# One order of matmul widths in every triple, and another way to fold the sample columns, in a one-core hybrid decoder step

## The chip, the core and the metric

The kernel runs on one core of one Trainium2 chip. TensorE (PE in the profile) multiplies, VectorE (DVE), ScalarE (ACT) and GpSimd (POOL) do everything else, and SyncE (SP) issues most of the DMAs. The metric is device microseconds of one execution, as a median over runs.

## What is computed

One layer of a decoder trunk is applied to 256 prompt tokens and 8 sample tokens (264 columns in all) with a model width of 2048. In fp32:

```
xn = rms_norm(x) ; z = xn @ w_in                      # 2048 -> 3584, columns split among three mixers
A: pooling over windows 2/4/8/16, a 128x128 map per group, @ w_pool_br
B: conv of width 4, RG-LRU (two 128x128 gate maps per block, a scan over time), * gelu gate, @ w_lru_br
C: GLU, conv of width 31, LayerNorm, silu, @ w_conf_br
x = x + (sum_b sigmoid(xn @ w_gate + b_gate)_b * y_b) @ w_out
x = x + relu(rms_norm(x) @ w_up)^2 @ w_down           # 2048 -> 8192 -> 2048
y = rms_norm(x)                                       # and the new mixer states
```

All of it is fp32, and every product is made from split operands, as the next section tells.

## The kernel before

**Layout.** Activations lie feature by feature: a k-tile is 128 features on the partitions and the 264 tokens along the row. `X` holds the residual stream. Every operand of a product is kept as a high part (the value rounded to fp32r) and a low part (the rest). Both lie side by side in one row, so `both(t, k)` is 528 columns wide: low prompt (0 to 255), low sample (256 to 263), high prompt (264 to 519), high sample (520 to 527). Low sample and high are thus neighbours.

**The triple.** A weight tile of 128x128 is also split, into `whi` and `wlo`. A product needs three matmuls: `whi` with the high activations, `whi` with the low ones, `wlo` with the high ones. `mm` and `mm3` (lines 234 to 242) make them so: k=0 is `whi` on columns 256 to 527 (low sample and all of high, 272 wide) into columns 0 to 271 of the PSUM bank; k=1 is `whi` on the low prompt (256 wide) into columns 8 to 263; k=2 is `wlo` on high (264 wide) into columns 8 to 271. So columns 8 to 271 of a bank hold the product, but for the product of the low sample part, which lies apart in columns 0 to 7. The order in a triple is 256, 272, 264. Only in the first triple of an accumulation is it 272, 256, 264, since the widest must clear the bank.

**Folding the sample columns.** `join` (line 158) adds columns 0 to 7 to the sample columns 264 to 271: ACT copies them to `side` in SBUF (L161), VectorE adds them back in PSUM (L162). Then the bank's consumer reads `tokens(ps)`, columns 8 to 271. Every accumulation has such a join, 288 in all.

**Order of the work.** The weights come as a list of chunks of 128x1024 (two k-tiles by 512 output features), in the order of `weight_plan`. A group is one weight matrix by 512 output features: 7 groups of w_in, 12 of w_gate, 4 each of w_pool_br, w_lru_br, w_conf_br and w_out, 16 of w_up and 16 of w_down, 67 in all. A group uses four PSUM banks, one for each of its four output tiles m, and the next group uses the other four. In each chunk the loops run over two k-tiles and four m, a triple each (`tile_mm`). The first four chunks go width by width instead (`by_operand`): four tiles with k=0, four with k=1, four with k=2. The small products are made between chunks: `lru_gate_mm` (four blocks of four products in "lru" chunks, with two sigmoids after each pair, L514 and L515) and `grp_mm` (four products, scaled by ACT in L767).

**Splitting of weights.** For chunk i+3 `split` is issued ahead of chunk i's matmuls: ACT casts `raw` to `whi` (L218), VectorE makes `wlo` from both (L219). `whi` and `wlo` have four buffers, `raw` six. Every engine works through its instructions in program order, so whatever an instruction waits for also delays the casts and subtractions queued behind it.

**Evacuation.** After a group's last chunk, for each m: `join`, then the consumer, for instance `gate_evac` (L792), `branch_evac` (L805, with additions on POOL in L808 and L811), `out_evac` (L831), `up_evac` (L866), `down_evac` (L892). Background stages (convolutions, gates, splits) are handed out between chunks by `run_bg` with a fixed credit for each engine; nothing in that depends on run time. The very last tile goes through `last_evac` (L888, L889), in two halves of 132 columns. Squares for the final norm are made by `square_add` on ACT (L854) and summed by POOL (L856), and the scaling by g_final is L897. The sums over the partitions are the matmuls of L1053.

Of the kernel before, what the change touches and what calls it, by code (L numbers as in the profile page):

```python
# [12 lines left out]
ALU = mybir.AluOpType  # L13
# [4 lines left out]
TP = 256  # L18
TS = 8
N = TP + TS  # L20
# [32 lines left out]
NHI = 4  # L53
# [38 lines left out]
def hybrid_step(ctx: ExitStack, tc: tile.TileContext, first, par_in, st_in, wall, y_out, st_out):  # L92
    nc = tc.nc
# [9 lines left out]
    whi = cpool.tile([P, NHI, CH], F32R, name="whi")  # L103
    wlo = cpool.tile([P, NHI, CH], F32R, name="wlo")
# [5 lines left out]
    L = cpool.tile([P, 8 * PITCH], F32R, name="L", tag="L")  # L110
    X = cpool.tile([P, KD, N], F32, name="X")
# [23 lines left out]
    def both(t, k):  # L135
        return part(t, k, 0, 2 * N)
# [16 lines left out]
    def tokens(ps):  # L153
        return ps[:, TS:TS + N]

    side, joined = cpool.tile([P, 4, TS], F32, name="side"), []

    def join(ps):
        t = side[:, len(joined) % 4, :]
        joined.append(t)  # L160
        nc.scalar.copy(t, ps[:, :TS])  # L161
        nc.vector.tensor_tensor(ps[:, N:N + TS], ps[:, N:N + TS], t, op=ALU.add)  # L162

    spare = nc.const_aps.tensor(1.0, [P, 2 * P], dtype=mybir.dt.bfloat16)
# [6 lines left out]
    groups, chunks = weight_plan()  # L171
# [59 lines left out]
        hi, lo, w = head_half(k, h)  # L231
        nc.vector.tensor_tensor(lo, w, f(hi), op=ALU.subtract)

    def mm(k, ps, w, x, start, stop=False):
        a, b = ((TP, 2 * N), (0, TP), (N, 2 * N))[k]
        o = (0, TS, TS)[k]
        nc.tensor.matmul(ps[:, o:o + b - a], w, x[:, a:b], start=start, stop=stop, skip_group_check=True)  # L237

    def mm3(ps, whi_t, wlo_t, x, first, last):
        for k in (0, 1) if first else (1, 0):  # L240
            mm(k, ps, whi_t, x, first and k == 0)
        mm(2, ps, wlo_t, x, False, last)

# [258 lines left out]
    def lru_gate_mm(ct, c, j):  # L504
        assert "xc" in done
        hi, lo = whi[:, c % NHI, :], wlo[:, c % NHI, :]
        out = []
        for t in range(2):
            s = slice((2 * j + t) * P, (2 * j + t + 1) * P)
            ps = acc()  # L510
            mm3(ps, hi[:, s], lo[:, s], both(L, ct), True, True)
            join(ps)
            out.append(ps)
        nc.scalar.activation(RA[:, ct, :], tokens(out[0]), AF.Sigmoid, bias=pv("b_lru_a", ct))  # L514
        nc.scalar.activation(TM[:, ct, :], tokens(out[1]), AF.Sigmoid, bias=pv("b_lru_x", ct))  # L515
        spend(act=1.0)
        if ct % 2:
            def times():
                nc.vector.tensor_tensor(XC[:, ct - 1:ct + 1, :], XC[:, ct - 1:ct + 1, :], TM[:, ct - 1:ct + 1, :],
                                        op=ALU.mult)  # L520
                spend(dve=0.71)

            later(1, times)
# [198 lines left out]
    def Q():  # L722
        if not q_at:
            q_at.append(cpool.tile([P, 8 * PITCH], F32R, name="Q", tag="Q"))
        return q_at[0]
# [33 lines left out]
    def grp_mm(c):  # L759
        assert "pool" in done  # L760
        hi, lo = whi[:, c % NHI, :], wlo[:, c % NHI, :]
        for gi in range(4):
            s = slice(gi * P, (gi + 1) * P)
            ps = acc()
            mm3(ps, hi[:, s], lo[:, s], both(Q(), gi), True, True)
            join(ps)
            nc.scalar.activation(DU[:, gi, :], tokens(ps), AF.Copy, scale=pv("pool_scale", gi))  # L767
        stage_split("pool", 2, lambda c: highs(Q(), 2 * c), lambda c: lows(Q(), 2 * c), lambda c: DU[:, 2 * c:2 * c + 2, :])
        mark("pool", "grp")
# [57 lines left out]

    sq2 = G[:, 20, :]

    def out_evac(m, ps):  # L830
        nc.vector.tensor_tensor(X[:, m, :], X[:, m, :], ps[:, :N], op=ALU.add)  # L831
        spend(dve=0.4)

        hi, lo = high(*bpart(m)), low(*bpart(m))

        def one():
            nc.scalar.activation(hi, X[:, m, :], AF.Copy, scale=pv("g_mlp", m))
            square_add(m)
            spend(act=0.8)

        def other():
            nc.vector.scalar_tensor_tensor(lo, X[:, m, :], pv("g_mlp", m), f(hi),
                                           op0=ALU.mult, op1=ALU.subtract)
            spend(dve=0.35)

        later(m % 4 // 2, one)
        later(m % 4 // 2 + 1, other)
        if m == KD - 1:
            later(4, lambda: total_fold(high(LH(), 0), G[:, 10, :], sq2))
            later(6, lambda: rms_close(high(LH(), 0)))  # L850
# [30 lines left out]
    def last_evac(whole):  # L881
        m = KD - 1
        for s in (slice(0, N // 2), slice(N // 2, N)):
            if s.start:
                join(whole)
            ps = tokens(whole)
            x = X[:, m, s]
            nc.vector.tensor_tensor(x, x, ps[:, s], op=ALU.add)  # L888
            nc.vector.tensor_tensor(G[:, 11, s], x, x, op=ALU.mult)  # L889

    def down_evac(q, m, ps):
        nc.vector.tensor_tensor(X[:, m, :], X[:, m, :], ps[:, :N], op=ALU.add)  # L892
        spend(dve=0.4)
        if q == 3:
            def rest():
                square_add(m, m < KD - 2)
                nc.scalar.activation(X[:, m, :], X[:, m, :], AF.Copy, scale=gfin[:, m:m + 1])  # L897

            later(0 if m >= KD - 4 else 1 + m % 4 // 2, rest)
# [51 lines left out]
    def by_operand(i, kt, rhs, pss):  # L951

        x = rhs(2 * i + kt)
        for k, w in enumerate((whi, whi, wlo)):
            for m in range(4):
                s = slice(kt * 512 + m * P, kt * 512 + (m + 1) * P)
                mm(k, pss[m], w[:, i % NHI, s], x, i == kt == k == 0)

    def tile_mm(i, c, kt, m, rhs, pss, stop):
        s = slice(kt * 512 + m * P, kt * 512 + (m + 1) * P)  # L960
        mm3(pss[m], whi[:, i % NHI, s], wlo[:, i % NHI, s], rhs(2 * c + kt), c == 0 and kt == 0, stop)


    for k in range(4):
# [13 lines left out]
    pss = None  # L978
    for i, ch in enumerate(chunks):
        now[0] = i  # L980
        if i < 5:
            x_tile(2 * i + 6)
            x_tile(2 * i + 7)
        for half in (0, 1) if i < 2 else (None,):
            split(i + AHEAD, half)
        if i == 12:
            softplus()
            again = first[:, KD:KD + 4 * HEAD].rearrange("p (k c) -> p k c", k=4)[:, :, :N]
            nc.sync.dma_start(X[:, 0:4, :], again)
            nc.vector.tensor_scalar(gfin, pv("g_final"), -0.5, None, op0=ALU.mult)  # L990
        if i % 2 == 0:
            dma_pair((i + 8) // 2)
        if i == 2:
            nc.sync.dma_start(par, par_in)
            nc.sync.dma_start(small(S_SMALL, S_IN - S_SMALL), st_in[:, S_SMALL:])
        if 13 <= i < 17:
            state_move(i - 13, lambda t, s: nc.sync.dma_start(t, st_in[:, s]))
        kind, gi, c, _ = ch
        if kind == "dense":
            rhs, fn = group(gi)  # L1000
            n = groups[gi][2] // 2
            if c == 0:
                pss = [acc() for _ in range(4)]
            if i < len(chunks) - 2:
                for kt in range(2):
                    if i < LEAD:
                        by_operand(i, kt, rhs, pss)
                    for m in range(4 * (i < LEAD), 4):
                        tile_mm(i, c, kt, m, rhs, pss, c == n - 1 and kt == 1)
            elif i == len(chunks) - 1:  # L1010
                for m in range(4):
                    for b in range(4):
                        tile_mm(i - 1 + b // 2, c - 1 + b // 2, b % 2, m, rhs, pss, b == 3)
            if c == n - 1:
                for m in range(4):
                    if (gi, m) == (len(groups) - 1, 3):
                        last_evac(pss[m])
                    else:
                        join(pss[m])
                        fn(m, tokens(pss[m]))  # L1020
                after(gi)
        elif kind == "lru":
            for j in range(2):
                lru_gate_mm(2 * gi + j, i, j)
            if gi == 3:
                lru_tail()
        elif kind == "grp":
            grp_mm(i)
        if i == len(chunks) - 4:
            nc.scalar.preload_act_table_set(ROOT)  # L1030
        if 136 <= i < 140:
            state_move(i - 136, lambda t, s: nc.sync.dma_start(st_out[:, s], t))
        if i == 140:
            nc.sync.dma_start(st_out[:, S_SMALL:], st)
        if 5 <= i < 9:
            x_squares(i - 5)
        if i == 9:
            later(0, x_sum)
        if i == 12:
            later(0, x_rms)  # L1040
        run_bg()
# [8 lines left out]
    ps = [acc(), acc()]  # L1050
# [139 lines left out]
```

## Time and profile before

| | us |
|---|---|
| median of 3 runs | 1386.58 (1385.03 to 1386.98) |
| the profiled execution | 1385.67 |
| its span, first to last instruction | 1383.9 |
| PE busy | 1367.4 (99%) |
| VectorE busy | 876.9 (63%) |
| ACT busy | 758.3 (55%) |
| GpSimd busy | 94.7 (7%) |

A row of the timeline view has the start and length in us, the engine, the line, the operation with output and inputs by the program's names, and a count where several were merged; in brackets stands the engine's idle time ahead of it and what ended that. A row of the groups of instructions has the busy time and the mean ns of one behind the first bar and the idle time behind the second. In the page's first part an engine's row has busy us, share of the span and instructions.

### The profile page before, as it was taken

The numbers are of one execution on the slowest core, as the hardware profiler recorded it, in microseconds if no ns is written. First come the engines' busy times: TensorE is split into PE (matmuls) and PEld (weight loads), VectorE is DVE, ScalarE is ACT, GpSimd is POOL, SyncE is SP. The second block draws the span as 40 slices with busy tenths as digits, with TensorE's granted clock in tenths as the row PEclk, the third lists the DMA queues.
The fourth block names the chain that finished last, engine by engine and source line by source line (L and its number), as shares of the span: only waits on it lengthen the run. The fifth ranks groups of instructions, "written<-read, shape, count | busy, mean of one in ns | idle before, by whom it ended". The sixth has DMA issues, their size and how long they took to land.

```text
span 1383.9 us, 27199 instructions
## 1 busy us (share of the span) xinstructions
PE 1367.4 (99%) x11421; PEld 1363.9 (99%) x11421; DVE 876.9 (63%) x1340; ACT 758.3 (55%) x1309; POOL 94.7 (7%) x125
## 2 busy tenths in 40 slices
PE   9999999999999999999999999999999999999996
PEld 9999999999999999999999999999999999999996
DVE  7786788776767668666655455655455655555554
ACT  7756667667665655555544344543344533454553
POOL 0230010110101013010000000000000000000012
PEclk9999999999999999999999999999999999999999
DMA  8654556555565554655555555555555555555551
GB/s 321 215 176 162 189 183 211 178 182 192 183 214 183 183 184 153 213 179 187 183 183 183 183 184 185 184 185 184 188 186 186 186 186 186 186 183 183 183 183 63
DMA packets 40826, 257.53 MB, mean 186 GB/s; under 512 B 4480, under 2 KB 6784, under 8 KB 11776
## 3 DMA queue, kind: packets, MB, share of 16 engines
q1 hardware_dynamic: 40272, 255.19, 53.7%
q8 instruction: 89, 1.46, 0.4%
q10 hardware_dynamic: 432, 0.61, 0.1%
q14 instruction: 33, 0.27, 0.1%
HBM read 252.57 MB, written 3.21 MB: 185 GB/s over the span
## 4 chain that ended last, share of the span: by engine, by line
PE 94%; DVE 3%; ACT 1%; POOL 1%; issue 1%; DMA 0%; DVEq 0%; ACTq 0%; POOLq 0%
PE acc L237 93%; DVE wlo L219 1%; ACT whi L218 1%; DVE A L821 1%; POOL G L811 0%; DMA tmp<-first_dram 0%; DVE y L1076 0%; DVE G L805 0%; DVE acc L162 0%; DVE tmp L585 0%; DVE L L501 0%; ACT tmp L515 0%; ACT G L767 0%; ACT tmp L535 0%; POOL G L856 0%
## 5 line engine op out<-in xcount | busy, mean ns | idle before, releaser
L219 DVE TENSOR_TENSOR wlo<-raw,whi 128x1024 fp32r<-128x1024 f32 (+1 forms) x478 | 582.7, 1222 | 466.4 <-ACT whi L218 465.2
L218 ACT CAST whi<-raw 128x1024 fp32r<-128x1024 f32 (+1 forms) x478 | 494.7, 1039 | 462.1 <-PE acc L237 420.5
L237 PE MATMUL acc<-A,whi 128*128 128x256 f32 (+1 forms) x3968 | 709.5, 282 | 1.7 <-ACT tmp L514 1.0
L237 PEld LDWEIGHTS acc<-A,whi 128*128 128x128 f32 x3968 | 608.7, 188 | 2.8 <-ACT tmp L514 1.6
L237 PE MATMUL acc<-A,wlo 128*128 128x264 f32 x1984 | 556.6, 283 | 2.1 <-DVE wlo L219 2.1
L237 PEld LDWEIGHTS acc<-A,wlo 128*128 128x128 f32 x1984 | 371.3, 188 | 2.9 <-DVE wlo L219 2.9
L237 PE MATMUL acc<-xn,whi 128*128 128x256 f32 (+1 forms) x2048 | 366.3, 281 | 0.0
L237 PEld LDWEIGHTS acc<-xn,whi 128*128 128x128 f32 x2048 | 314.6, 188 | 0.0
L237 PE MATMUL acc<-xn,wlo 128*128 128x264 f32 x1024 | 288.8, 282 | 0.0
L237 PEld LDWEIGHTS acc<-xn,wlo 128*128 128x128 f32 x1024 | 192.3, 188 | 0.0
L237 PE MATMUL acc<-Q,whi 128*128 128x272 f32 (+1 forms) x776 | 139.4, 281 | 0.0
L237 PE MATMUL acc<-LH,whi 128*128 128x272 f32 (+1 forms) x768 | 138.1, 282 | 0.0
L237 PEld LDWEIGHTS acc<-Q,whi 128*128 128x128 f32 x776 | 119.2, 188 | 0.0
L237 PEld LDWEIGHTS acc<-LH,whi 128*128 128x128 f32 x768 | 118.1, 188 | 0.0
L237 PE MATMUL acc<-Q,wlo 128*128 128x264 f32 x388 | 109.5, 282 | 0.0
L237 PE MATMUL acc<-LH,wlo 128*128 128x264 f32 x384 | 108.4, 282 | 0.0
L161 ACT COPY side<-acc 128x8 f32<-128x8 f32 x288 | 45.0, 166 | 92.5 <-PE acc L237 89.8
L856 POOL TENSOR_TENSOR G<-G 128x264 f32<-128x264 f32 x28 | 26.7, 953 | 793.2 <-ACT G L854 792.1
L237 PEld LDWEIGHTS acc<-Q,wlo 128*128 128x128 f32 x388 | 72.9, 188 | 0.0
L237 PEld LDWEIGHTS acc<-LH,wlo 128*128 128x128 f32 x384 | 72.1, 188 | 0.0
L635 ACT ACTIVATE G<-tmp,par 128x256 f32<-128x256 f32 x120 | 54.4, 501 | 6.5 <-DVE G L638 5.6
L162 DVE TENSOR_TENSOR acc<-acc,side 128x8 f32<-128x8 f32 x288 | 47.2, 166 | 12.1 <-ACT side L161 12.1
(184 smaller groups left out, 592.0 us busy)
## 6 DMA issues: line engine op xcount, KB each, us to landing
raw<-wall_dram SPq DMA_DIRECT2D x226, 1024.0 KB, 4.9
raw<-wall_dram SPq DMA_DIRECT2D x12, 512.0 KB, 6.1
raw<-first_dram SPq DMA_DIRECT2D x6, 512.0 KB, 8.1
X<-first_dram SPq DMA_DIRECT2D x6, 264.0 KB, 7.7
raw<-wall_dram SPq DMA_DIRECT2D x5, 256.0 KB, 2.9
tmp<-first_dram SPq DMA_DIRECT2D x3, 388.0 KB, 4.3
y_dram<-y SPq DMA_DIRECT2D x3, 264.0 KB, 2.2
tmp<-st_dram SPq DMA_DIRECT2D x4, 188.0 KB, 5.0
```

Of the source, the lines that this page charges most:

```text
L161: nc.scalar.copy(t, ps[:, :TS])
L162: nc.vector.tensor_tensor(ps[:, N:N + TS], ps[:, N:N + TS], t, op=ALU.add)
L218: nc.scalar.copy(h[:, s], r[:, s])
L219: nc.vector.tensor_tensor(lo[:, s], r[:, s], f(h[:, s]), op=ALU.subtract)
L237: nc.tensor.matmul(ps[:, o:o + b - a], w, x[:, a:b], start=start, stop=stop, skip_group_check=True)
L635: nc.scalar.activation(dst[:, ct, :TP], vext[:, ct, k:k + TP], AF.Copy, scale=par[:, w:w + 1])
L821: nc.vector.tensor_tensor(lo, x, f(hi), op=ALU.subtract)
L856: nc.gpsimd.tensor_tensor(sq2, sq2, t, op=ALU.add)
```

## The change

`mm` no longer has three fixed kinds. It takes a tuple: whether the weight is `wlo`, and the columns of the activations. Two lists of three such tuples exist. `MIXED` is 272 (`whi`), 264 (`wlo`), 256 (`whi`), in this order in every triple, first or not. `ALIKE` is 264 (`whi` on high), 264 (`wlo` on high), 264 (`whi` on all of low); here the low sample product goes straight into the sample columns, so nothing has to be folded. `ALIKE` is used in the first group and in the small products (no join there any more), `MIXED` in all other groups.

Where a fold is still needed it goes one of three ways. In the other groups of w_in `join` is as it was (copy by ACT). In w_gate, the three branch projections and w_up VectorE does the copy too. In w_out and w_down there is no join: the whole product is added to `X`, then columns 0 to 7 are added to the sample columns of `X` (`add_side`), also in `last_evac`.

```diff
-    def join(ps):
+    def join(ps, by_act):
         t = side[:, len(joined) % 4, :]
         joined.append(t)
-        nc.scalar.copy(t, ps[:, :TS])
+        if by_act:
+            nc.scalar.copy(t, ps[:, :TS])
+        else:
+            nc.vector.tensor_copy(t, ps[:, :TS])
         nc.vector.tensor_tensor(ps[:, N:N + TS], ps[:, N:N + TS], t, op=ALU.add)
...
-    def mm(k, ps, w, x, start, stop=False):
-        a, b = ((TP, 2 * N), (0, TP), (N, 2 * N))[k]
-        o = (0, TS, TS)[k]
-        nc.tensor.matmul(ps[:, o:o + b - a], w, x[:, a:b], start=start, stop=stop, skip_group_check=True)
-
-    def mm3(ps, whi_t, wlo_t, x, first, last):
-        for k in (0, 1) if first else (1, 0):
-            mm(k, ps, whi_t, x, first and k == 0)
-        mm(2, ps, wlo_t, x, False, last)
+    ALIKE = (False, N, 2 * N), (True, N, 2 * N), (False, 0, N)
+    MIXED = (False, TP, 2 * N), (True, N, 2 * N), (False, 0, TP)
+
+    def mm(ps, hi, lo, x, what, start, stop=False):
+        low_w, a, b = what
+        o = TS + N - (b - a) if b > N else TS
+        nc.tensor.matmul(ps[:, o:o + b - a], lo if low_w else hi, x[:, a:b], start=start, stop=stop,
+                         skip_group_check=True)
+
+    def mm3(ps, hi, lo, x, first, last, form):
+        for k in range(3):
+            mm(ps, hi, lo, x, form[k], first and k == 0, last and k == 2)
...
-            mm3(ps, hi[:, s], lo[:, s], both(L, ct), True, True)
-            join(ps)
+            mm3(ps, hi[:, s], lo[:, s], both(L, ct), True, True, ALIKE)
...
-            mm3(ps, hi[:, s], lo[:, s], both(Q(), gi), True, True)
-            join(ps)
+            mm3(ps, hi[:, s], lo[:, s], both(Q(), gi), True, True, ALIKE)
...
-    def out_evac(m, ps):
-        nc.vector.tensor_tensor(X[:, m, :], X[:, m, :], ps[:, :N], op=ALU.add)
+    def out_evac(m, whole):
+        into_x(m, whole)
...
     def last_evac(whole):
         m = KD - 1
         for s in (slice(0, N // 2), slice(N // 2, N)):
+            x = X[:, m, s]
+            nc.vector.tensor_tensor(x, x, tokens(whole)[:, s], op=ALU.add)
             if s.start:
-                join(whole)
-            ps = tokens(whole)
-            x = X[:, m, s]
-            nc.vector.tensor_tensor(x, x, ps[:, s], op=ALU.add)
+                add_side(m, whole)
             nc.vector.tensor_tensor(G[:, 11, s], x, x, op=ALU.mult)
 
-    def down_evac(q, m, ps):
-        nc.vector.tensor_tensor(X[:, m, :], X[:, m, :], ps[:, :N], op=ALU.add)
+    def add_side(m, whole):
+        x = X[:, m, TP:]
+        nc.vector.tensor_tensor(x, x, whole[:, :TS], op=ALU.add)
+
+    def into_x(m, whole):
+        nc.vector.tensor_tensor(X[:, m, :], X[:, m, :], tokens(whole), op=ALU.add)
+        add_side(m, whole)
+
+    def down_evac(q, m, whole):
+        into_x(m, whole)
...
-        for k, w in enumerate((whi, whi, wlo)):
+        for k in (0, 2, 1):
             for m in range(4):
                 s = slice(kt * 512 + m * P, kt * 512 + (m + 1) * P)
-                mm(k, pss[m], w[:, i % NHI, s], x, i == kt == k == 0)
+                mm(pss[m], whi[:, i % NHI, s], wlo[:, i % NHI, s], x, ALIKE[k], i == kt == k == 0)
...
-                        tile_mm(i, c, kt, m, rhs, pss, c == n - 1 and kt == 1)
+                        tile_mm(i, c, kt, m, rhs, pss, c == n - 1 and kt == 1,
+                                    MIXED if gi else ALIKE)
...
-                        join(pss[m])
-                        fn(m, tokens(pss[m]))
+                        if gi and name not in ("w_out", "w_down"):
+                            join(pss[m], name == "w_in")
+                        fn(m, pss[m] if name in ("w_out", "w_down") else tokens(pss[m]))
```

More of the change, by code (lines that the diff above doesn't have):

```diff
@@ L953, in by_operand, with tile_mm @@
         x = rhs(2 * i + kt)
-        for k, w in enumerate((whi, whi, wlo)):
+        for k in (0, 2, 1):
             for m in range(4):
                 s = slice(kt * 512 + m * P, kt * 512 + (m + 1) * P)
-                mm(k, pss[m], w[:, i % NHI, s], x, i == kt == k == 0)
-    def tile_mm(i, c, kt, m, rhs, pss, stop):
+                mm(pss[m], whi[:, i % NHI, s], wlo[:, i % NHI, s], x, ALIKE[k], i == kt == k == 0)
+    def tile_mm(i, c, kt, m, rhs, pss, stop, form=MIXED):
         s = slice(kt * 512 + m * P, kt * 512 + (m + 1) * P)
-        mm3(pss[m], whi[:, i % NHI, s], wlo[:, i % NHI, s], rhs(2 * c + kt), c == 0 and kt == 0, stop)
+        mm3(pss[m], whi[:, i % NHI, s], wlo[:, i % NHI, s], rhs(2 * c + kt), c == 0 and kt == 0, stop,
+            form)
     for k in range(4):
@@ L1000, in hybrid_step @@
             rhs, fn = group(gi)
+            name = groups[gi][0]
             n = groups[gi][2] // 2
```

## The prediction

> **What bounds the kernel now.** First the page: how busy each engine is, then its chain that ended last.
>
> ```profile
> span 1383.9 us, 27199 instructions
> PE 1367.4 (99%) x11421; PEld 1363.9 (99%) x11421; DVE 876.9 (63%) x1340; ACT 758.3 (55%) x1309; POOL 94.7 (7%) x125
> PE 94%; DVE 3%; ACT 1%; POOL 1%; issue 1%; DMA 0%; DVEq 0%; ACTq 0%; POOLq 0%
> ```
>
> PE is the bound nearly everywhere. So the time is the number of matmuls by their spacing, plus the few places where PE stands still, plus what follows the last weight. The change removes no column of a matmul: 272+264+256 and 3x264 are both 792. It can only move spacing, stops and tail. For the stops I read the waits of PE in the timeline:
>
> ```profile
> 5.04 0.79 PE L237 MATMUL acc<-A,whi 128*128 128x272 f32 x2 [0.48 <-DVE A L355]
> 112.82 0.39 PE L237 MATMUL acc<-A,wlo 128*128 128x264 f32 x1 [0.29 <-DVE wlo L219]
> 128.51 0.51 PE L237 MATMUL acc<-A,whi 128*128 128x272 f32 x2 [1.04 <-ACT tmp L514]
> 141.64 0.39 PE L237 MATMUL acc<-A,wlo 128*128 128x264 f32 x1 [0.75 <-DVE wlo L219]
> 195.83 0.39 PE L237 MATMUL acc<-A,wlo 128*128 128x264 f32 x1 [0.74 <-DVE wlo L219]
> 555.24 0.39 PE L237 MATMUL acc<-A,wlo 128*128 128x264 f32 x1 [0.29 <-DVE wlo L219]
> 1372.96 1.62 PE L1053 MATMUL acc<-G,ones 128*128 128x132 f32 x12 [2.65 <-POOL G L856]
> ```
>
> A bracket undercounts a stop: idle time begins at the end of a 0.28 us matmul, but the next would have started 0.12 after its start, so 0.16 more is lost, and the matmul after the stop is 0.11 longer (0.39). The five stops from 112.82 to 555.24 thus cost 0.56, 1.31, 1.02, 1.01 and 0.56.
>
> **The change, part by part.**
>
> *One order of widths.* Starts of `wlo` matmuls, each a triple's last; a group begins right after 683.63:
>
> ```profile
> 8.06 0.65 PE L237 MATMUL acc<-A,wlo 128*128 128x264 f32 x4
> ...
> 16.80 0.65 PE L237 MATMUL acc<-A,wlo 128*128 128x264 f32 x4
> ...
> 683.63 0.28 PE L237 MATMUL acc<-xn,wlo 128*128 128x264 f32 x1
> ...
> 685.09 0.28 PE L237 MATMUL acc<-xn,wlo 128*128 128x264 f32 x1
> ...
> 686.54 0.28 PE L237 MATMUL acc<-xn,wlo 128*128 128x264 f32 x1
> ...
> 689.39 0.28 PE L237 MATMUL acc<-xn,wlo 128*128 128x264 f32 x1
> ```
>
> From 686.54 eight triples take 2.85 (118.8 ns a matmul). The eight from the group's start take 2.91: four in the order 272, 256, 264 take 1.46 (121.7 ns), and the four after them, back in the usual order, still take 1.45. So a broken order costs 0.06 a group, and the fast rhythm needs some triples to come back. Is it the evacuation of the group before that slows PE there? The first group speaks against it: there nothing is evacuated, the widths come in runs of four equal ones, and six rounds of twelve take 16.80-8.06=8.74, 121.4 ns a matmul. I take the order as the cause. Repeated without a break, 272, 264, 256 is the same ring as 256, 272, 264, with the same weight kind and columns at each width; only the boundary between tiles m has moved. So I expect the fast rhythm throughout and no breaks: 66 groups after the first by 0.05 to 0.06, -3.5. Bounds: nothing gained; or, in all 3712 MIXED triples, the slow 121.7 in place of 118.8, +32; or, below, the same step the other way, -32, for which no row speaks. I take the middle because the ring is the same.
>
> In sentences of its own: the Trainium skill ("TensorE: Matmul & The Clock Gate", Back-to-back issue gap) gives the isolated gap as N/2.4 + 2.5 ns, a sum over widths in which order has no place. By it this term is 0. The trace disagrees: the same three widths took 2.91 and 2.85.
>
> *Equal widths.* In the first group 32 triples outside `by_operand` go from 118.8 to, if equal widths cost as there, 121.4 ns: 96 x 2.6 ns = +0.25. Between ends of -0.25 (as much better than the rhythm as the row is worse) and +0.3 (121.7) I take the row. The rest of that group and the small products lose an irregular order and get equal widths, 0.
>
> *Small products without joins.* From 104 to 131 us:
>
> ```profile
> L219 DVE TENSOR_TENSOR wlo<-raw,whi 128x1024 fp32r<-128x1024 f32 (+1 forms) x11 | 11.7, 1074 | 5.3 <-ACT whi L218 5.3
> L514 ACT ACTIVATE tmp<-acc,par 128x264 f32<-128x264 f32 x8 | 3.8, 481 | 9.7 <-DVE acc L162 9.7
> ...
> 111.54 1.22 DVE L219 TENSOR_TENSOR wlo<-raw,whi 128x1024 fp32r<-128x1024 f32 x1 [1.77 <-ACT whi L218]
> ...
> 136.23 0.92 ACT L535 ACTIVATE tmp<-tmp,sp 128x264 f32<-128x264 f32 x2 [1.69 <-DVE G L519]
> ...
> 189.71 0.48 ACT L767 ACTIVATE G<-acc,par 128x264 f32<-128x264 f32 x1 [1.32 <-DVE acc L162]
> ```
>
> ACT copies, then its sigmoid waits 9.7 us in all for the VectorE addition, which sits behind a `wlo` subtraction; ACT's casts queue behind the sigmoid, and VectorE in turn waits for the casts. PE stops at 112.82 (late `wlo`) and at 128.51 (banks not read). Without joins the sigmoids start when PE is done, so ACT wins over 2 us a block, more than each stop. In the pool product ACT loses 1.32 plus three rounds of copy, addition and scaling; the stop at 195.83 is 1.01. The one at 141.64 belongs to the same backlog, since sigmoids feed L519 and L535. Gone: 0.56 + 1.31 + 0.4 (a second bank wait at 129.6, too short for a bracket) + 1.02 + 1.01 = -4.3. Bounds 0 (every stop replaced) and -4.5. PE coming 2 to 4 us earlier eats part of what ACT won; late next is the table load and L538 after 137.
>
> `wlo` is now second in a triple, not third, so a late `wlo` leaves one matmul more behind it: +0.12 wherever a stop stays.
>
> *VectorE copies in 40 groups* (12 w_gate, 12 branch, 16 w_up). A small operation:
>
> ```profile
> L454 DVE TENSOR_TENSOR st<-acc,rstd 128x8 f32<-128x8 f32 x4 | 0.7, 164 | 0.0
> ...
> L219 DVE TENSOR_TENSOR wlo<-raw,whi 128x1024 fp32r<-128x1024 f32 (+1 forms) x478 | 582.7, 1222 | 466.4 <-ACT whi L218 465.2
> ```
>
> 160 copies by 0.2 (164 ns and a gap, as between L162 and L805 below) are 32 us of VectorE, under the 466 us it idles ahead of L219. Not in w_conf_br:
>
> ```profile
> 542.30 0.16 DVE L162 TENSOR_TENSOR acc<-acc,side 128x8 f32<-128x8 f32 x1
> 542.50 0.43 DVE L805 TENSOR_TENSOR G<-acc,G 128x264 f32<-128x264 f32 x1
> ...
> 544.49 2.59 DVE L821 TENSOR_TENSOR A<-G,A 128x264 fp32r<-128x264 f32 x4
> 547.00 2.35 DVE L219 TENSOR_TENSOR wlo<-raw,whi 128x1024 fp32r<-128x1024 f32 x2
> 549.27 0.16 DVE L162 TENSOR_TENSOR acc<-acc,side 128x8 f32<-128x8 f32 x1
> ...
> 556.24 1.45 DVE L821 TENSOR_TENSOR A<-G,A 128x264 fp32r<-128x264 f32 x4
> ...
> 543.01 3.09 POOL L811 TENSOR_TENSOR G<-G,tmp 128x264 f32<-128x264 f32 x4 [3.88 <-DVE acc L162]
> ```
>
> A round lasts 6.97 (542.30 to 549.27) with VectorE never idle, against 48 matmuls x 0.119 = 5.7 on PE, and its lag ends in the stop at 555.24. Four copies add 0.8 a round, and what waits is `wlo`, queued behind them. But L821 takes 2.59 beside POOL and 1.45 without it; with additions spaced by 0.75 instead of 0.55, POOL finishes more of its work under VectorE's PSUM phase, and L821 then runs less slowed: I take 0.3 a round. In a sentence of its own: the Trainium skill ("SBUF — State Buffer", two separate sides) has VectorE and GpSimd lock a shared port pair for a whole instruction, and 2.59 against 1.45 agrees. Three rounds, 0.2 at their start and 0.12 for the order: +1.2 (between 0.1 and 3.0).
>
> *w_out, w_down.* The addition to `X` and `add_side` replace join and addition: two VectorE operations as before, one of ACT's fewer. 0 until the last tile:
>
> ```profile
> 1370.35 0.29 DVE L888 TENSOR_TENSOR X<-X,acc 128x132 f32<-128x132 f32 x1 [0.59 <-PE acc L237]
> 1370.67 0.29 DVE L889 TENSOR_TENSOR G<-X 128x132 f32<-128x132 f32 x1
> ...
> 1370.67 0.17 ACT L161 COPY side<-acc 128x8 f32<-128x8 f32 x1 [1.59 <-DVE X L888]
> 1370.73 0.43 ACT L854 ACTIVATE G<-X 128x264 f32<-128x264 f32 x1
> ...
> 1371.30 1.60 POOL L856 TENSOR_TENSOR G<-G 128x264 f32<-128x264 f32 x2 [17.19 <-ACT G L854]
> ```
>
> The squares of tiles 12 to 14 are queued on ACT behind the last tile's copy, which waits for PE's end; POOL's two sums follow, and PE's L1053 waits until 1372.96. Without joins ACT squares each tile as it comes, and POOL is done before PE ends. Then L1053 waits for L889 alone: its first half is ready at 1370.97, the second at some 1371.7 (addition, small addition and square by 0.2 to 0.3 each). Twelve L1053 in 1.62 us start 0.12 apart, two for each of three summands of a half, so the fifth, the first that needs L889, began at about 1373.5; now it can at 1371.05: -2.4 (bounds -1.2, where the second half binds all, and -2.6).
>
> *Start.* The first matmul reads no low part now, so it waits for L350 instead of L355:
>
> ```profile
> 4.40 0.49 DVE L355 SCALAR_TENSOR_TENSOR A<-tmp,A 128x264 fp32r<-128x264 f32 x1
> ```
>
> 0.5 earlier, at half speed, since the first two take 0.79: -0.3 (0 to -0.5).
>
> No DMA is issued more, fewer or elsewhere; SP's order is untouched.
>
> **Sum.** -3.5 +0.25 -4.3 +1.2 -2.4 -0.3 = -9.1 against the profiled execution's 1385.67, so 1376.6. That execution lies 0.9 under the median of 1386.58, and by the median it is 1377.5.
>
> **The rivals.**
>
> *Order is indifferent.* Group starts are slow for another reason (the bank cleared, the evacuation beside it) and stay so: 1377.5 + 3.5 = 1381. For it: only the first group separates the two.
>
> *The moved boundary spoils the rhythm, and it is slower.* The step from 256 to 272 now changes bank and weight tile, that from 264 to 256 no longer does. If PE needs them where they were, every triple runs at 121.7 and 11,136 matmuls by 2.9 ns cost +32: 1381 + 32 = 1413. It decides from 5.6 us in 11,136 matmuls, 0.5 ns each. Against it: the runs of equal widths, which change bank at each matmul, and the broken triples, which do not, go at 121.4 and 121.7, so banks seem not to matter.
>
> *VectorE becomes the bound in w_conf_br.* POOL gives nothing back, 0.8 a round and more lag at w_out's first chunks: +3 above the forecast, 1380.5.
>
> *The stops after the gates move on instead of going:* half of 4.3 stays, 1379.7.
>
> **How the numbers follow.** The forecast has 0.60 (own range 1374 to 1380.5), indifferent order 0.15, VectorE 0.08, moved stops 0.07, spoiled rhythm 0.10. The range 1373.5 to 1383 holds all but the last and some edges. A measurement of this kernel tells about 0.2% (2.8 us) from no change. Faster by more (under 1383.8): 0.87. Within: 0.03. Slower: 0.10, all from the spoiled rhythm.
>
> **What would show it.** Right: `wlo` starts 2.85 apart over eight triples also right after a group's start; no idle bracket on PE between 100 and 200 us; one of 0.7 to 1.5 near 550; L1053 at about 1.1 after PE's last weight matmul instead of 2.9; no L161 outside w_in. Wrong: 2.90 or more in the middle of w_down (spoiled), 2.91 still at group starts (indifferent), brackets that reappear on `wlo` after 137 or in several places from 530 to 560.

## The result, and the profile after

The changed kernel takes 1375.73 us (median of 6, 1375.28 to 1376.09), the kernel before in the same comparison 1386.78 (median of 6, 1385.03 to 1388.27). The ratio is 0.9921, with a 95% interval of 0.9908 to 0.9934: 11.05 us less. The forecast was 1377.5, or 9.1 less. The profiled execution took 1375.75 with a span of 1374.0, against 1385.67 and 1383.9. The page of the changed kernel (engines' busy time, chain that ended last):

```profile
span 1374.0 us, 26885 instructions
PE 1362.1 (99%) x11421; PEld 1359.9 (99%) x11421; DVE 894.1 (65%) x1476; ACT 725.8 (53%) x1045; POOL 95.5 (7%) x125
PE 97%; DVE 2%; issue 0%; ACT 0%; DVEq 0%
```

Both programs issue the same 11,421 matmuls, so the two traces can be laid over each other by matmul number, counted from 0. The table gives the start of a matmul in each:

| up to | before, us | after, us | gained in this part |
|---|---|---|---|
| first weight matmul (no. 17) | 5.04 | 4.60 | -0.44 |
| end of the first group (no. 209) | 28.72 | 28.27 | -0.01 |
| ahead of the gate products (no. 880) | 109.00 | 108.49 | -0.05 |
| behind the pool product (no. 1650) | 205.77 | 200.19 | -5.08 |
| in w_conf_br, ahead of its stops (no. 4400) | 534.43 | 527.19 | -1.66 |
| in w_out, behind them (no. 4700) | 570.82 | 564.95 | +1.37 |
| last weight matmul (no. 11408) | 1370.03 | 1362.47 | -1.69 |
| end of the span | 1383.90 | 1373.96 | -2.38 |

The idle times of PE that are left, from the timeline of PE in the changed kernel (the first row stands for the start):

```profile
4.60 1.21 PE L243 MATMUL acc<-A,whi 128*128 128x264 f32 x4
...
542.03 0.39 PE L243 MATMUL acc<-A,wlo 128*128 128x264 f32 x1 [0.29 <-DVE wlo L222]
549.27 0.39 PE L243 MATMUL acc<-A,wlo 128*128 128x264 f32 x1 [1.25 <-DVE wlo L222]
1363.46 1.22 PE L1068 MATMUL acc<-G,ones 128*128 128x132 f32 x8 [0.26 <-DVE G L892]
```

Nothing between 100 and 200 us, two stops where one was, and 0.26 instead of 2.65 in front of the last sums. ACT's sigmoids (L519, L520) and VectorE's subtraction, groups of instructions from 104 to 128 us:

```profile
L520 ACT ACTIVATE tmp<-acc,par 128x264 f32<-128x264 f32 x8 | 3.8, 480 | 0.0
L519 ACT ACTIVATE tmp<-acc,par 128x264 f32<-128x264 f32 x8 | 3.8, 480 | 1.2 <-PE acc L243 1.2
...
L222 DVE TENSOR_TENSOR wlo<-raw,whi 128x1024 fp32r<-128x1024 f32 (+1 forms) x12 | 12.9, 1090 | 7.9 <-ACT whi L221 7.9
```

The 9.7 us that the sigmoids waited for VectorE are 1.2 us for PE itself. A group starts right after 677.55 here; starts of `wlo`, eight triples apart:

```profile
677.55 0.28 PE L243 MATMUL acc<-xn,wlo 128*128 128x264 f32 x1
...
680.41 0.28 PE L243 MATMUL acc<-xn,wlo 128*128 128x264 f32 x1
...
683.26 0.28 PE L243 MATMUL acc<-xn,wlo 128*128 128x264 f32 x1
```

2.86 and 2.85: the start of a group is as fast as its middle. But not everywhere. From 28 to 42 us, and then at 60, four triples each:

```profile
36.09 0.29 PE L243 MATMUL acc<-A,wlo 128*128 128x264 f32 x1
...
37.56 0.29 PE L243 MATMUL acc<-A,wlo 128*128 128x264 f32 x1
...
59.95 0.28 PE L243 MATMUL acc<-A,wlo 128*128 128x264 f32 x1
...
61.37 0.28 PE L243 MATMUL acc<-A,wlo 128*128 128x264 f32 x1
```

1.47 and 1.42 for the same instructions in the same order: 122.2 and 118.9 ns a matmul over longer stretches. PE has two lasting rhythms. Counted from the start of a `wlo` matmul, the slow one repeats with every triple (122, 119, 126 ns from start to start), the fast one with every second triple (122, 112, 121, 119, 117, 123 ns). The kernel before has the slow one too, from 43 to 52, 443 to 454 and 466 to 477 us. There each slow stretch begins right behind a norm's single matmul (at 43.0, 442.0 and 465.3 us) and ends at the next group's broken order.

The w_conf_br round (VectorE's timeline, then POOL's):

```profile
535.79 0.15 DVE L164 COPY side<-acc 128x8 f32<-128x8 f32 x1
535.98 0.17 DVE L165 TENSOR_TENSOR acc<-acc,side 128x8 f32<-128x8 f32 x1
536.19 0.43 DVE L809 TENSOR_TENSOR G<-acc,G 128x264 f32<-128x264 f32 x1
...
538.79 2.05 DVE L825 TENSOR_TENSOR A<-G,A 128x264 fp32r<-128x264 f32 x4
540.76 2.35 DVE L222 TENSOR_TENSOR wlo<-raw,whi 128x1024 fp32r<-128x1024 f32 x2
543.03 0.15 DVE L164 COPY side<-acc 128x8 f32<-128x8 f32 x1
...
536.70 3.16 POOL L815 TENSOR_TENSOR G<-G,tmp 128x264 f32<-128x264 f32 x4 [4.08 <-DVE side L164]
```

A round takes 7.24 instead of 6.97: four copies add 0.8, and the four subtractions that POOL slows take 2.05 instead of 2.59. The tail, in the timelines of POOL, ACT and VectorE:

```profile
1361.22 0.76 POOL L860 TENSOR_TENSOR G<-G 128x264 f32<-128x264 f32 x1 [0.67 <-ACT G L858]
...
1362.08 0.42 ACT L858 ACTIVATE G<-X 128x264 f32<-128x264 f32 x1 [0.46 <-DVE X L896]
...
1363.12 0.29 DVE L892 TENSOR_TENSOR G<-X 128x132 f32<-128x132 f32 x1
...
1364.00 0.37 ACT L1075 ACTIVATE rstd<-acc,eps 128x132 f32<-128x132 f32 x1 [0.94 <-PE acc L1068]
```

POOL's sums end at 1361.98, before PE's last weight matmul (1362.47), and the fifth of the last sums waits for VectorE's half tile alone.

### The profile page after: what moved, and what is told of

Same layout as the page of the kernel before. It is cut to its first block, busy times and chain, and to the rows that moved or that the text cites. A ratio compares the mean times of both kernels' runs of the same rounds, so it can differ in the third digit from the quotient of the medians.

```text
span 1374.0 us, 26885 instructions
## 1 busy us (share of the span) xinstructions
PE 1362.1 (99%) x11421; PEld 1359.9 (99%) x11421; DVE 894.1 (65%) x1476; ACT 725.8 (53%) x1045; POOL 95.5 (7%) x125
## 4 chain that ended last, share of the span: by engine, by line
PE 97%; DVE 2%; issue 0%; ACT 0%; DVEq 0%
PE acc L243 97%; DVE wlo L222 1%; DVE A L825 0%; DVE G L809 0%; PE acc L340 0%; DVE y L1091 0%; DVE acc L165 0%; ACT whi L221 0%; DVE side L164 0%; DVE acc L1082 0%; DVEq L1182 0%; DVE G L1081 0%; DVE acc L1080 0%; PE acc L1068 0%; PE acc L323 0%
## 5 line engine op out<-in xcount | busy, mean ns | idle before, releaser
L243 PE MATMUL acc<-A,whi 128*128 128x256 f32 (+2 forms) x3968 | 709.0, 281 | 0.0
L243 PE MATMUL acc<-xn,whi 128*128 128x272 f32 (+1 forms) x2048 | 366.0, 281 | 0.0
L243 PE MATMUL acc<-Q,whi 128*128 128x256 f32 (+2 forms) x776 | 140.7, 281 | 0.0
L643 DVE TENSOR_TENSOR G<-G 128x1024 f32<-128x1024 f32 x30 | 38.2, 1274 | 0.0
L899 DVE TENSOR_TENSOR X<-X,acc 128x264 f32<-128x264 f32 x79 | 33.4, 423 | 6.4 <-PE acc L243 6.4
```

What stands on the lines that cost most here:

```text
L243: nc.tensor.matmul(ps[:, o:o + b - a], lo if low_w else hi, x[:, a:b], start=start, stop=stop, skip_group_check=True)
L643: nc.vector.tensor_tensor(VC[:, :, :TP], VC[:, :, :TP], src[:, :, :TP], op=ALU.add)
L899: nc.vector.tensor_tensor(X[:, m, :], X[:, m, :], tokens(whole), op=ALU.add)
```

## The experiments

All were timed against the kernel before on the same chip. The changed kernel was not run again beside them: its 1375.73 comes from the comparison above, where the kernel before took 1386.78, and beside the experiments that took 1385.73, 1386.31 and 1386.61. Differences of about 1 us to the changed kernel therefore rest on the traces. The theory at the start was that of the prediction: a broken order at group starts costs, the joins of the small products make PE's stops, the last copy holds back the tail, and VectorE's copies lengthen w_conf_br.

**The order alone, in the kernel before.**

```diff
     def mm3(ps, whi_t, wlo_t, x, first, last):
-        for k in (0, 1) if first else (1, 0):
-            mm(k, ps, whi_t, x, first and k == 0)
-        mm(2, ps, wlo_t, x, False, last)
+        mm(0, ps, whi_t, x, first)
+        mm(2, ps, wlo_t, x, False)
+        mm(1, ps, whi_t, x, False, last)
```

> The kernel before with nothing changed but the order: 272, 264, 256 in every triple, first or not; all joins by ACT as before. Theory 'the broken order costs': eight triples take 2.85 us right after a group's start too, 66 groups save about 0.05 each, -3.3, and a late wlo leaves one matmul more behind each of the four stops, +0.5: -2.8 against the kernel before. Rival 'order is indifferent': group starts stay at 2.91, the time moves by 0 to +0.5. Rival 'the moved boundary between tiles spoils the rhythm': +32.

Median 1383.67 of eleven, against 1385.73: -2.1. Eight lie between 1382.60 and 1384.22 and three between 1389.54 and 1391.32, so the ratio over all of them shows no gain (0.9995, 0.9981 to 1.001). No trace of one of the three exists; 6.6 us would be some 2,000 matmuls in the slow rhythm, but that is not shown. In the trace of a run at 1383.95 the order does what the theory said, by the number of matmuls begun within 800 to 1000 us in the kernel before, the changed one and this one (busy us, count, granted clock):

```profile
800.00:1000.00 200.00, 200.00 (x1681) 1.00 0.54 185
```

```profile
800.00:1000.00 200.00, 200.00 (x1685) 1.00 0.54 185
```

```profile
800.00:1000.00 200.00, 200.00 (x1685) 1.00 0.54 185
```

The last weight matmul starts 3.04 earlier than before. The stops stay and grow, as the earlier `wlo` has it (0.87 where 0.29 was). And 1.3 us are lost in the tail. The timeline of PE:

```profile
112.54 0.39 PE L237 MATMUL acc<-A,wlo 128*128 128x264 f32 x1 [0.87 <-DVE wlo L219]
...
1369.92 3.01 PE L1053 MATMUL acc<-G,ones 128*128 128x132 f32 x12 [2.65 <-POOL G L856]
```

The last twelve matmuls of it in a window of their own (busy us, count, granted clock):

```profile
1369.90:1373.00 3.10, 3.01 (x12) 0.52 0.00 0
```

In the kernel before, the twelve took 1.62 after a stop of the same length, at a granted clock of 1.00. Here the clock fell to about half.

**The break put back, in the changed kernel.**

```diff
-        for k in range(3):
+        for k in (0, 2, 1) if first else (0, 1, 2):
             mm(ps, hi, lo, x, form[k], first and k == 0, last and k == 2)
```

> The changed kernel with one thing undone: in the first triple of an accumulation the order is 272, 256, 264 again. Theory 'the broken order costs': +3.3 against the changed kernel (1375.7), so about 1379, with 2.91 for the eight triples after a group's start. Rival 'order is indifferent': 1375.7.

1389.14: 13.4 above the changed kernel, four times what was expected, and above even the kernel before (ratio 1.0024, 1.0015 to 1.0033). Starts of `wlo`, 24 triples apart, in two neighbouring groups:

```profile
666.51 0.28 PE L243 MATMUL acc<-xn,wlo 128*128 128x264 f32 x1
...
675.07 0.28 PE L243 MATMUL acc<-xn,wlo 128*128 128x264 f32 x1
...
689.49 0.29 PE L243 MATMUL acc<-xn,wlo 128*128 128x264 f32 x1
...
698.29 0.29 PE L243 MATMUL acc<-xn,wlo 128*128 128x264 f32 x1
```

8.56 and 8.80. One group runs in the fast rhythm, the next in the slow one from its start to its end; from 685 us on it is every third group. About 3,570 matmuls of this trace lie in slow stretches, and 3,570 by 3.3 ns are 11.9 us. The theory "a break costs 0.05" falls short: here a break also chooses the rhythm until the next one. This break is not quite that of the kernel before, where a 264 stands ahead of its first 272 and a 256 behind its last 264; here these neighbours are 256 and 272. In the trace of the kernel before no break led into the slow rhythm.

**The ring the other way.**

```diff
-    MIXED = (False, TP, 2 * N), (True, N, 2 * N), (False, 0, TP)
+    MIXED = (False, TP, 2 * N), (False, 0, TP), (True, N, 2 * N)
```

> The changed kernel with the ring run the other way: 272, 256, 264 in every triple, first or not, so no order is ever broken either. Theory A, 'only a break costs, any fixed order is fast': 118.9 ns a matmul and 1375.7. Theory B, 'the fast rhythm belongs to the ring 272, 264, 256': this order ran at 121.7 at the group starts of before, 11,136 matmuls by 2.9 ns are +32, 1408.

1408.51 (ratio 1.0142, 1.0106 to 1.0177), theory B to half a microsecond; one of four executions took 1396.2. PE in the same window:

```profile
800.00:1000.00 200.00, 200.00 (x1638) 1.00 0.52 179
```

200 us by 1638 is 122.1 ns a matmul. An order that is never broken is not enough: 272, 256, 264 is mostly slow, at the full clock, with the same widths, weights and instructions. It has two rhythms as well, 122.2 and 120.0 ns: from 125 to 187 us (between a gate product and the pool product) and from 445 to 468 us (between two norms' single matmuls) it ran at 120.0. It ran faster nowhere, taken over 24 matmuls. Whether the execution of 1396.2 spent longer at 120.0 is not known, since it has no trace.

**Three equal widths everywhere**, so that nothing is folded (also without `add_side`).

```diff
-                        tile_mm(i, c, kt, m, rhs, pss, c == n - 1 and kt == 1,
-                                    MIXED if gi else ALIKE)
+                        tile_mm(i, c, kt, m, rhs, pss, c == n - 1 and kt == 1,
+                                    ALIKE)
...
-                        if gi and name not in ("w_out", "w_down"):
-                            join(pss[m], name == "w_in")
```

> The changed kernel with three widths of 264 in every triple of every group, so that no sample columns have to be folded anywhere (no join, no add_side). The first group's last four chunks ran at 120.0 ns a matmul so in the changed kernel's trace: 11,136 matmuls by 1.1 ns are +12.4, and the two stops near 545 us (2.1) should go: about +10, 1386. Rival 'the folds cost more than the rhythm': at or under 1375.7. Rival 'equal widths find a faster rhythm when the run is long' (118.9): 1373.5.

1404.24 (ratio 1.0133, 1.0117 to 1.0148), 28.5 above the changed kernel. All expectations missed:

```profile
800.00:1000.00 200.00, 200.00 (x1646) 1.00 0.52 182
```

From 43 us on, where the first norm's single matmul comes between, equal widths run at 121.7, not at the 120.0 up to there: 11,136 by 2.8 ns are +31, and the stops near 545 us, which are gone with the folds, give back 2. So equal widths have more than one rhythm too, and the fold is far cheaper than leaving the ring.

**w_conf_br joined by ACT again.**

```diff
-                            join(pss[m], name == "w_in")
+                            join(pss[m], name in ("w_in", "w_conf_br"))
```

> The changed kernel with one thing undone: in the four w_conf_br groups ACT copies the sample columns again, as before. Theory 'the sixteen VectorE copies lengthen VectorE's rounds there': the stops near 542 and 549 us (2.1 together) shrink to the one of the kernel before (0.6): -1.5, so 1374.2. Rival 'the lag there comes from elsewhere, such as the earlier need of wlo': 1375.7.

1374.86 (ratio 0.9917, 0.9902 to 0.9931), 0.9 below the changed kernel, which the time alone can't tell apart; by matmul numbers this stretch is 1.08 shorter. One wait of 0.7 on `wlo` is left:

```profile
PE acc L243 <- DVE wlo L222: 0.7, 1, 0.7
```

The copies are most of that loss; a stop like the one of the kernel before remains.

**w_conf_br with equal widths and no join.**

```diff
-                                    MIXED if gi else ALIKE)
+                                    MIXED if gi and name != "w_conf_br" else ALIKE)
...
-                        if gi and name not in ("w_out", "w_down"):
+                        if gi and name not in ("w_out", "w_down", "w_conf_br"):
```

> The changed kernel with three widths of 264 and no join at all in the four w_conf_br groups. VectorE is spared 32 small operations, so the stops near 545 us go (-2.1); 384 matmuls at 120.0 to 121.7 ns cost +0.4 to +1.1. If PE then falls back to the rhythm of 118.9 at once: 1374 to 1374.7. If it stays in the slow rhythm of 122.2 that the changed kernel showed from 28 to 42 us after its equal widths, until something breaks it (a single matmul between the groups near 640 us): 768 matmuls by 3.3 ns, +2.5 more, about 1377.

1373.88 (ratio 0.9910, 0.9895 to 0.9925), 1.9 below the changed kernel; by matmul numbers the stretch from no. 4304 to 4700 is 1.56 shorter. The expectation counted 384 matmuls in w_conf_br, but the four groups have 192, so that the widths cost +0.2 to +0.5; the trace has +0.53, and the stops that went gave back 2.1. The only wait of PE on another engine between the first and the last weight matmul is this, in the view of its waits:

```profile
PE acc L243 <- ACT whi L231: 0.3, 1, 0.3
```

In w_conf_br PE runs at 120 to 121.7, and w_out is fast at once. In four short groups, where VectorE is the bound, leaving the ring pays.

**The small products joined by ACT again**, with mixed widths in the new order.

```diff
-            mm3(ps, hi[:, s], lo[:, s], both(L, ct), True, True, ALIKE)
+            mm3(ps, hi[:, s], lo[:, s], both(L, ct), True, True, MIXED)
+            join(ps, True)
...
-            mm3(ps, hi[:, s], lo[:, s], both(Q(), gi), True, True, ALIKE)
+            mm3(ps, hi[:, s], lo[:, s], both(Q(), gi), True, True, MIXED)
+            join(ps, True)
```

> The changed kernel with the small products undone: mixed widths and a join with a copy by ACT for the sixteen gate products and the four pool products. Theory 'ACT waits behind these joins make the stops of PE between 110 and 200 us': they return, +4.5 to +5, about 1380.5. Rival 'the ring alone removed them, or they came from the table loads': 1375.7. A wlo that is late leaves one matmul more behind it, +0.1 a stop.

1381.42, 5.7 above the changed kernel; by matmul numbers its trace is 0.4 us ahead of the changed kernel's at no. 880, 5.4 behind at no. 1650 and 5.4 behind at the end, so the loss arises in the small products alone, 5.8 us. Some 0.3 of it are slow rhythm between the stops, from 124 to 140 us. The stops are back in the timeline of PE:

```profile
112.39 0.39 PE L243 MATMUL acc<-A,wlo 128*128 128x264 f32 x1 [0.87 <-DVE wlo L222]
...
128.08 0.39 PE L243 MATMUL acc<-A,whi 128*128 128x272 f32 x1 [0.98 <-ACT tmp L520]
...
141.22 0.39 PE L243 MATMUL acc<-A,wlo 128*128 128x264 f32 x1 [0.59 <-DVE wlo L222]
```

**The last four tiles joined by ACT**, added to `X` as before.

```diff
+        if last:
+            join(whole, True)
         nc.vector.tensor_tensor(X[:, m, :], X[:, m, :], tokens(whole), op=ALU.add)
-        add_side(m, whole)
+        if not last:
+            add_side(m, whole)
...
-        into_x(m, whole)
+        into_x(m, whole, q == 3 and m >= KD - 4)
...
             if s.start:
-                add_side(m, whole)
+                join(whole, True)
```

(In `last_evac` the join again stands in front of the second half's addition.)

> The changed kernel with the last four tiles undone: join with a copy by ACT in front of the addition to X for tiles 12 to 15, as before. Theory 'the last copy holds ACT's squares back': L1068's counterpart of L1053 waits for POOL again, 2.9 us after the last weight matmul, +2.4, about 1378.1. Rival 'the tail is set by the halves of the last tile': 1375.7.

1378.70, 3.0 above the changed kernel; the trace loses 2.9 behind the last weight matmul. The wait for POOL is back at its old length, in the timeline of PE:

```profile
1365.72 2.15 PE L1071 MATMUL acc<-G,ones 128*128 128x132 f32 x12 [2.65 <-POOL G L860]
```

and the granted clock over the twelve sums is 0.71:

```profile
1365.70:1368.00 2.30, 2.15 (x12) 0.71 0.00 0
```

**One matmul more.** Built on the kernel with equal widths in w_conf_br.

```diff
+                    if gi == 1 and (c, kt) == (1, 0):
+                        nc.tensor.matmul(pss[0][:, TS + N:], whi[:, i % NHI, :P], rhs(2)[:, N:N + 512 - TS - N],
+                                         start=False, stop=False, skip_group_check=True)
```

> The kernel with equal widths in w_conf_br (1373.9) and one matmul more, 240 wide, in the second chunk of the second group, into 240 PSUM columns that nothing reads. In that group PE ran at 122.2 ns a matmul from 28 to 42 us, until the one matmul of the first norm came between. Theory 'PE has two lasting rhythms for one and the same order, and one matmul between is enough to choose anew': the stretch after the extra one runs at 118.9, -0.3 to -0.4 with its own 0.11, 1373.5. Rival 'the slow stretch has a cause in that place, such as the other engines' load while the first weights arrive': still 122.2 until 42 us, 1374.0.

The slow stretch ends at the extra matmul (L1020). Timeline of PE:

```profile
30.49 0.29 PE L243 MATMUL acc<-A,wlo 128*128 128x264 f32 x1
30.85 0.29 PE L243 MATMUL acc<-A,wlo 128*128 128x264 f32 x1
31.09 0.28 PE L1020 MATMUL acc<-A,whi 128*128 128x240 f32 x1
31.34 0.28 PE L243 MATMUL acc<-A,wlo 128*128 128x264 f32 x1
31.70 0.28 PE L243 MATMUL acc<-A,wlo 128*128 128x264 f32 x1
```

It was 122.2 ns a matmul ahead and is 118.9 behind, at a place where the kernel without it stays slow until 42.8 us. The rival that the place makes it slow falls. The time, 1373.66 (ratio 0.9903, 0.9888 to 0.9918), is too near to 1373.88 to be told apart by the clock alone. It is the fastest kernel of this study.

**The same in each of the last 32 groups** (`gi >= 35` in place of `gi == 1`).

> The same extra matmul in the second chunk of each of the last 32 groups (w_up, w_down), where PE runs at 118.9 throughout. Their own time is 32 x 0.11 = +3.5, 1377.4. Theory A, 'the fast rhythm is taken up again after any disturbance of it': 118.9 behind each, 1377.4 to 1378.5. Theory B, 'each extra matmul switches between the two rhythms': half of the groups at 122.2, 16 x 192 x 3.3 ns are +10 more, 1388. Theory C, 'it falls one way or the other by something that the program doesn't show': between these, with slow stretches that begin and end at extra matmuls.

1378.61, 4.7 above its base. Behind 31 of the 32 PE is at 118.9 again; behind the first, at 633 us, it runs at 122.2 until another single matmul (that of the second norm) at 648. Theory B falls. A is nearly right, and the one exception is what C allows.

## Why the prediction was right, point by point

*One order, -3.5.* The size was right: over 35 groups from no. 4700 to the last the gain is 1.69, or 0.048 a group, and all parts away from the stops add up to about -3.4. Some 0.8 of this are the slow stretches of the kernel before, 256 matmuls by 3.3 ns, which the forecast had not seen and which are gone; 0.4 are lost again from 28 to 43 us. The reason was half of it. A group start costs because it breaks a ring, as said; that the ring is one of two, and that PE holds a slow or a fast rhythm in it until something disturbs it, was not seen. The reversed ring shows that the order counts, the extra matmul that the rhythm can be chosen anew. "The middle because the ring is the same" held, but with luck: the same ring would have cost 3.3 ns more in each of 11,136 matmuls, +37, if PE had kept the slow rhythm that it held until 43 us. The isolated gap that the Trainium skill gives for a matmul ("TensorE: Matmul & The Clock Gate", Back-to-back issue gap) goes by the width alone and has no room for this: the same instructions took 118.9 and 122.2 ns, and the reversed ring mostly 122.1.

*Equal widths, +0.25.* Not seen: the first group took as long as before (-0.01), since its rounds ran at 120.5 and 120.0 instead of 121.4 and 118.9. What was missed is behind it: from equal widths PE came into the slow rhythm for 14 us, +0.4.

*Small products, -4.3.* Measured -5.08 up to no. 1650, of which the stops are 4.9. Two stops that the forecast had left out, 0.24 at 123.6 and 0.34 at 194.6, went with the others, and none came back. Undoing this part alone gave back 5.7.

*w_conf_br, +1.2.* Measured +1.37 with the order's gain in the same groups in it; the stops themselves went from 0.56 to 2.08, +1.5. The give-back from POOL came as said (0.27 a round in place of 0.8), so that rival falls. The stop is now two, since the first chunk of w_out is late as well.

*Tail, -2.4.* Measured -2.38. Undoing it cost 3.0. In its trace it cost 2.9, of which 0.5 are the clock, which fell there: the last twelve sums took 2.15 in place of 1.62.

*Start, -0.3.* Measured -0.44 at the first weight matmul. Other runs of the same instructions start up to 0.26 earlier or 0.22 later (4.34 and 4.82), so half of it is within what a run can do.

*Sum.* -9.94 in the profiles against -9.1. By the medians it is -11.05. The last microsecond isn't in the two profiles. Executions of the kernel before spread over 3.2 us and those of the changed one over 0.8; a tail stop after which the clock sometimes falls, and stops that choose a rhythm, would do that, but this is argued, not shown.

*The rivals.* Indifferent order: refuted by both rings. Spoiled rhythm: it didn't happen to this change, but a kernel that is slow nearly throughout costs about what it said; the reversed ring, a different change, cost 32.8 where 32 had been worked out. VectorE as bound with nothing given back by POOL, and stops moving on: neither.

## What to carry to other kernels

When one engine is busy 99% of the time, measure its spacing in several stretches before calling it fixed: matmuls of the same columns in sum ran at 118.9, 120.0, 121.7 and 122.2 ns here, by nothing but the widths, their order and what had come before, and 32 us hang on that. Look for what queues behind a short instruction that waits for another engine: the copies of eight columns in the small products, 0.17 us each, held up 5 us of PE's work in all, and the same copy in the tail 2.4. Moving such a copy to another engine is right only where that engine has room; in w_conf_br it had none, and leaving the copy out altogether was worth 1.6 in the trace and 1.9 by the medians.

## What the runs showed of the hardware

Two rhythms of one instruction stream were not expected. With 272, 264, 256 PE lasts in 118.9 or in 122.2 ns a matmul, at a granted clock of 1.00 in both. It keeps whichever it is in, the fast one over 5,998 matmuls at the end of the changed kernel, until a break in the order, a stop or a single other matmul. The slow one never had so long a run here: a break, a stop or a single matmul came within some 190. What then decides between them stays open. 31 of 32 extra matmuls left the fast one as it was, but behind three of the four single matmuls of norms in the kernel before PE was in the slow one. Of the broken group starts, every third led to the slow one in the kernel with the break put back, from 685 us on, and none in the kernel before. Nor is it settled why 272, 256, 264 is mostly slow.

A stop of 2.65 us in the tail left the granted clock at 1.00 (kernel before), 0.71 and 0.52 in three traces, and the twelve matmuls behind it took 1.62, 2.15 and 3.01. In the clock records of these traces the granted clock changes only between 1.00 and 0.50, and only in steps of 3.41 us: with the order alone it falls at 1369.47, rises at 1372.88 and falls at 1376.30; in the kernel before, the first rise and the next fall lie 1372.16 apart, 402 steps. It fell where PE had been idle for 2.2 us (order alone) and 2.5 us (tail joined) of the step that ended, and not after steps with 1.2 and 1.8 us idle (kernel before). In the view of windows, the step ahead of the fall and the one behind it, with the order alone (busy us, count, granted clock):

```profile
1366.06:1369.47 3.41, 1.21 (x11) 1.00 0.00 0
1369.48:1372.87 3.39, 2.95 (x12) 0.50 0.00 0
```

In these traces, then, where the steps fall against the stop decides what the stop costs. The Trainium skill ("TensorE: Matmul & The Clock Gate", What's actually happening) has a gate that halves the clock after an idle window of about 3.4 us that runs freely. The length of the steps agrees with that; but a stop of 2.65 us, shorter than the window, was enough for a fall in two of three traces.
